# A ring of weight slots at a pitch of 2080 bytes in place of 2048, in a hybrid decoder layer

## The chip, the cores and the metric

The kernel runs on one core of a Trainium2 chip. The engines are named as the profile names them: PE is TensorE with its matmuls (PEld its weight loads), ACT is ScalarE, DVE is VectorE, POOL is GpSimd, SP is the engine that issues most transfers. The metric is the device time of one execution in microseconds; lower is better.

## The reference

One layer of a decoder trunk for 512 positions and a model width of 1024, in float32. A short gated convolution and a gated delta rule run side by side, are merged by sigmoid gates, and a gated feed-forward part with a convolution follows.

```python
h = rmsnorm(x, norm_mix_g)
proj = h @ w_in                                   # 1024 -> nine groups of 1024, and a, b
bg, cg, xv, q, k, v, z, a, b, ga, gb = split(proj)
y_a = (bg * causal_dwconv(cg * xv, conv_a_w)) @ w_a_out
y_b = gdn_branch(q, k, v, z, a, b, ...) @ w_b_out # conv, silu, chunked delta rule, norm, silu(z)
x = x + (sigmoid(ga) * y_a + sigmoid(gb) * y_b) @ w_o
h = rmsnorm(x, norm_ffn_g)
up = causal_dwconv(h @ w_up, ffn_conv_w)          # 1024 -> 2 x 2816
gate, val = split(up)
x = x + (silu(gate) * val) @ w_down
return rmsnorm(x, norm_final_g)
```

## The kernel before

Every large product is split in three. A float32 operand is taken apart into a rounded part, of type float32r, and the remainder; `mm3` sums hi x lo, lo x hi and hi x hi in one bank of PSUM. All of these matmuls are recorded by the helper `mm`, line 108, so line 108 stands for nearly the whole of the kernel's arithmetic. In a row of the profile such as `ps<-hT,wh` the first operand after the arrow is the moving one, the second the stationary one (it is loaded by a LDWEIGHTS of its own).

The activations of a stage lie in SBUF in both parts for the stage's whole length: hT (normalised input, two tiles for the two parts), ts and us (sums and differences of blocks of it, 256 columns wide), yas and yb (the two mixers' outputs), h (the normalised input of the feed-forward part), mix and xs (inputs of the last two products). Weights are streamed. A `Block` is one transfer of 1 MB into one of two `raw` buffers. `Block.part` makes of a quarter of it (128 partitions by 512 elements, 2048 bytes a partition) a rounded copy `wh` on ACT (line 140) and a remainder `wl` on DVE (line 141). wh and wl come from rings of WQ = 12 slots each, in the tile pool `wp`. In the projections the ring's slots are the stationary operand, 128 columns (512 bytes) at a time; in the products with w_o and w_down a slot is the moving operand with all its 512 columns. Some blocks are used by a seven-product scheme (`SumBlock`, L161 and `sum_job`), with products of 256 columns on ts or us.

The order is written out by hand: `run_jobs` goes through a list of jobs, splits the next block while the matmuls of the present one run, and every 4 x 512 columns `tick` advances queues of small steps (evictions, convolutions, the delta rule). A convolution (`conv`, L335 and L338) writes to a buffer named cv: ACT copies the PSUM bank into it, scaled, DVE adds three shifted taps, ACT reads it back through Silu (L973). Three cv buffers are in the pool `gd`; one of them serves `gates_chain` first, under the name abT.

Addresses follow from the order in which the pools hand out space from the bottom of a partition. `const` comes first, with `gate`, a small tile that POOL writes to; then `wp` with raw, the slots of wh and those of wl; then hp (hT, yb), gs, gd, or fp (h) in their place later. The pool `sc` and the later `up` (ts, us, yas, mix, xs) are set from the other end of the partition. `before` and `after` in this table are the byte at which a buffer begins in a partition, in the built program, and behind it what is left on division by 128:

| buffer | before | after |
|---|---|---|
| ident, in const | 1216 (64) | 1248 (96) |
| raw | 2848, 11040 (32) | 2880, 11072 (64) |
| wh, 12 slots | 19232, 21280, 23328, 25376 ... (32 each) | 19264, 21344, 23424, 25504 ... (64, 96, 0, 32, and so on) |
| wl, 12 slots | 43808, 45856 ... (32 each) | 44224, 46304 ... (64, 96, 0, 32, and so on) |
| hT, both parts; later yb in both parts | 68384, 84768 (32) | 69184, 85568 (64) |
| h, both parts | 84768, 101152 (32) | 85568, 101952 (64) |
| ts, yas, mix | 135136, 151520 (96) | the same |
| us, xs | 151520, 167904 (96) | the same |

Within hT, yb and h the k-tiles stand 2048 bytes apart, so each begins at the same remainder; halves of 256 columns do too, and so do ts, us and xs in their steps of 1024 or 512 bytes.

Of the kernel before, what the change touches and what calls it, by code (L numbers as in the profile page):

```python
# [9 lines left out]
F32 = mybir.dt.float32  # L10
F32R = mybir.dt.float32r
# [5 lines left out]
P = 128  # L17
S = 512
# [13 lines left out]
WQ = 12  # L32
# [28 lines left out]
def layer_kernel(ctx, tc, x, norm_mix_g, w_in, w_ab, conv_a_w, gdn_conv_w, gdn_A_log, gdn_dt_bias,  # L61
# [9 lines left out]
    const = ctx.enter_context(tc.tile_pool(name="const", bufs=1))  # L71
    wp = ctx.enter_context(tc.tile_pool(name="wp", bufs=2))
# [3 lines left out]
    def nm(s):  # L76
        cnt[0] += 1
        return f"{s}{cnt[0]}"

    def bank():  # L80
        return ps.tile([P, 512], F32, tag="ps", name=nm("ps"))
# [40 lines left out]
            mm(o, ah, bh, False, i == n - 1, free)  # L122


    class Block:
        def __init__(self, src, quarter=(4, P)):
            self.src, self.quarter = src, quarter
            self.raw, self.ready, self.lead, self.fed = None, False, 2, True
            self.wh, self.wl = {}, {}
# [5 lines left out]
            nc.sync.dma_start(out=self.raw, in_=self.src())  # L135

        def part(self, name, src):
            wh = self.wh[name] = wp.tile([P, *self.quarter], F32R, tag="wh", bufs=WQ, name=nm("wh"))
            wl = self.wl[name] = wp.tile([P, *self.quarter], F32R, tag="wl", bufs=WQ, name=nm("wl"))
            act.copy(out=wh, in_=src)  # L140
            dve.tensor_tensor(out=wl, in0=src, in1=wh.bitcast(F32), op=ALU.subtract)  # L141

# [73 lines left out]
            use(block.wh, block.wl)  # L216


    gate = const.tile([1, 16], F32, name="gate")

    def feed(raw):
        el = raw[0:1, 1].rearrange("p k n -> p (k n)") if len(raw.shape) == 4 else raw[0:1, 1]
# [152 lines left out]
    k_block = Block(lambda: w_in[C_K])  # L375
# [51 lines left out]
    with tc.tile_pool(name="st1", bufs=1) as st1:  # L427
# [83 lines left out]
                                     op0=ALU.mult, op1=ALU.subtract)  # L511

        def round_k(q):
            wh = k_block.wh[q] = wp.tile([P, 4, P], F32R, tag="wh", bufs=WQ, name=nm("wh"))
            act.copy(out=wh, in_=k_block.raw[:, q])

        def rest_k(q):
            wl = k_block.wl[q] = wp.tile([P, 4, P], F32R, tag="wl", bufs=WQ, name=nm("wl"))
            dve.tensor_tensor(out=wl, in0=k_block.raw[:, q], in1=k_block.wh[q].bitcast(F32), op=ALU.subtract)


# [68 lines left out]
    gd = p2.enter_context(tc.tile_pool(name="gd", bufs=1))  # L590

    def hn(ap):
        return ap.rearrange("p (h n) -> p h n", n=NT)

    def prep(pr):
        Dm = gd.tile([P, 8, P], F32, tag="Dm", name=nm("Dm"))
        nc.sync.dma_start(out=Dm, in_=gtd[8 * pr:8 * pr + 8, :].partition_broadcast(P))
        pool.affine_select(out=Dm, in_=Dm, compare_op=ALU.is_ge, fill=-1e30, base=0,
                           pattern=[[0, 8], [1, P]], channel_multiplier=-1)
        Dms[pr] = Dm  # L600
# [8 lines left out]
    Dms = {}  # L609

    def gates_chain(o):
        abT = gd.tile([P, S], F32, tag="cv", bufs=3, name="abT")[0:32]
        act.copy(out=abT, in_=o[0:32, :])
        yield
        o2 = bank()
        for n in range(NT):
            pe.transpose(out=o2[:, n * 32:(n + 1) * 32], in_=abT[:, n * P:(n + 1) * P], identity=ident[:32, :32])
        ab4 = o2[:, 0:128].rearrange("p (n c) -> p c n", c=32)
        abv = gd.tile([P, 16, NT], F32, name="abv")
        dve.tensor_copy(out=abv, in_=ab4[:, 16:32])  # L620
        dve.tensor_tensor(out=abv, in0=abv, in1=ab4[:, 0:16], op=ALU.add)
        T = lambda n: gd.tile([P, 32], F32, tag=n, name=nm(n))
        u, t, z, q, g = T("u"), T("t"), T("z"), T("q"), T("g")
        dve.tensor_tensor(out=hn(u), in0=abv[:, 0:8, :], in1=dtb.unsqueeze(2).broadcast_to([P, H, NT]), op=ALU.add)
        tc.keep_in_program_order(act.activation(out=hn(beta), in_=abv[:, 8:16, :], func=AF.Exp, scale=-1.0))
        tc.keep_in_program_order(act.activation(out=alg, in_=alg, func=AF.Exp))
        dve.tensor_scalar(t, u, -1.0, None, op0=ALU.mult)
        dve.tensor_tensor(out=t, in0=t, in1=u, op=ALU.min)
        tc.keep_in_program_order(act.activation(out=t, in_=t, func=AF.Exp))
        yield  # L630
        pool.tensor_scalar(beta, beta, 1.0, None, op0=ALU.add)
        pool.tensor_scalar(z, t, 2.0, None, op0=ALU.add)
        yield
        dve.reciprocal(out=beta, in_=beta)
        dve.reciprocal(out=z, in_=z)
        dve.tensor_scalar(u, u, 0.0, None, op0=ALU.max)
        yield
        pool.tensor_tensor(out=t, in0=t, in1=z, op=ALU.mult)
        pool.tensor_tensor(out=z, in0=t, in1=t, op=ALU.mult)
        pool.tensor_scalar(q, z, 1.0 / 15.0, 1.0 / 13.0, op0=ALU.mult, op1=ALU.add)  # L640
        for c in (11, 9, 7, 5, 3, 1):
            pool.tensor_tensor(out=q, in0=q, in1=z, op=ALU.mult)
            pool.tensor_scalar(q, q, 1.0 / c, None, op0=ALU.add)
        pool.tensor_tensor(out=q, in0=q, in1=t, op=ALU.mult)
        pool.tensor_scalar(q, q, 2.0, None, op0=ALU.mult)
        pool.tensor_tensor(out=g, in0=q, in1=u, op=ALU.add)
        pool.tensor_tensor(out=hn(g), in0=hn(g), in1=alg.unsqueeze(2).broadcast_to([P, H, NT]), op=ALU.mult)
        pool.tensor_scalar(g, g, -1.0, None, op0=ALU.mult)
        for _ in range(Y_G):
            yield  # L650
        o3 = bank()
        pe.matmul(o3[:, 0:32], lhsT=triu, rhs=g, start=True, stop=True)
        pe.matmul(o3[:, 32:64], lhsT=ones, rhs=g, start=True, stop=True)
        G, Gl = T("G"), T("Gl")
        dve.tensor_copy(out=G, in_=o3[:, 0:32])
        dve.tensor_copy(out=Gl, in_=o3[:, 32:64])
        dve.tensor_scalar(negG, G, -1.0, None, op0=ALU.mult)
        dve.tensor_tensor(out=kdv, in0=Gl, in1=G, op=ALU.subtract)
        act.activation(out=kdv, in_=kdv, func=AF.Exp)
        act.activation(out=eGl, in_=Gl, func=AF.Exp)  # L660
        act.activation(out=eG, in_=G, func=AF.Exp)
        dve.tensor_scalar(neG, eG, -1.0, None, op0=ALU.mult)
        yield
        o4 = bank()
        pe.transpose(out=o4[0:32, 0:P], in_=G, identity=ident)
        GT = gd.tile([32, P], F32, name="GT")
        dve.tensor_copy(out=GT, in_=o4[0:32, 0:P])
        nc.sync.dma_start(out=gtd, in_=GT)
        prep(0)
# [288 lines left out]
    def pair_jobs(pr):  # L958
        st = {}

        def qkv(which, j, o):
            c = gd.tile([P, S], F32, tag="cv", bufs=3, name=nm("cv"))
            yield from conv(c, o, gdn_w(which * 8 + 2 * pr + j), 4)
            if which == 1 and j == 0:
                reach(pr - 2, 99)
                st["kq"] = gd.tile([P, 2, 2, S], F32, tag="kq", bufs=2, name=nm("kq"))
                st["kqs"] = hp.tile([P, 2, 2, 2, S], F32R, tag="s", name=nm("kqs"))
            if which == 2 and j == 0:
                if pr:
                    ftask[pr - 1].until(VREAD)  # L970
                st["vT"] = gd.tile([P, 2, S], F32, tag="vT", name=nm("vT"))
            dst = (lambda: st["kq"][:, j, 1, :], lambda: st["kq"][:, j, 0, :], lambda: st["vT"][:, j, :])[which]()
            act.activation(out=dst, in_=c, func=AF.Silu)  # L973
            yield
            if which < 2:
                hi, lo = (st["kqs"][:, i, j, 1 - which, :] for i in range(2))
                act.copy(out=hi, in_=dst)
                dve.tensor_tensor(out=lo, in0=dst, in1=hi.bitcast(F32), op=ALU.subtract)
                yield
            if which == 2 and j == 1:  # L980
                st["v"] = True
            if which == 0 and j == 1:
                ftask[pr] = Task(front(pr, st))
                chains.append(ftask[pr])

        def zc(j, o):
            act.activation(out=yb[:, 2 * pr + j, :], in_=o, func=AF.Silu)
            if j == 1:
                st["z"] = True
            yield  # L990

        def first_k(wh, wl):
            use_ab()
            for j in range(2):
                products(o_k[j], wh, wl, j, hT, HS, S)
                evacs.append(Task(qkv(1, j, o_k[j])))

        return [(k_block, first_k) if pr == 0 else col_job(w_in, C_K + pr, hT, lambda j, o: qkv(1, j, o)),
                col_job(w_in, C_Q + pr, hT, lambda j, o: qkv(0, j, o)),
                col_job(w_in, C_V + pr, hT, lambda j, o: qkv(2, j, o)),  # L1000
                col_job(w_in, C_Z + pr, hT, zc)]
# [675 lines left out]
```

## Time and profile before

| | |
|---|---|
| three runs | 964.16, 964.42 and 3432.96 us |
| median of the runs | 964.42 us |
| the profiled execution, its own time | 964.32 us |
| its span, first to last instruction | 962.4 us |
| granted TensorE clock, mean | 0.998 of full |

Stages, by the span: the input norm and first projections up to about 25 us; projections for the delta rule beside its chain up to about 340 us; the short convolution's projections on hT and ts up to about 480 us; the two mixers' output products (yas, yb) up to about 595 us; the product with w_o and the second norm up to about 630 us; the feed-forward projections on h and us up to about 848 us; the product with w_down to the end.

In a row of instruction groups stand: line, engine, operation, output<-inputs by the program's names, their sizes, the count; behind the bar the busy time and the mean duration in ns; behind the second bar the idle time of that engine just before them and what ended it. In the timeline a row is the start, the time that it lasts, and how many equal neighbours were merged. Matmuls overlap and their ends are modelled, so their durations are longer than the distance from one start to the next.

### The profile page before, as it was taken

The numbers are of one execution on the slowest core, as the hardware profiler recorded it, in microseconds if no ns is written. First come the engines' busy times: TensorE is split into PE (matmuls) and PEld (weight loads), VectorE is DVE, ScalarE is ACT, GpSimd is POOL, SyncE is SP. The second block draws the span as 40 slices with busy tenths as digits, with TensorE's granted clock in tenths as the row PEclk, the third lists the DMA queues.
The fourth block names the chain that finished last, engine by engine and source line by source line (L and its number), as shares of the span: only waits on it lengthen the run. The fifth ranks groups of instructions, "written<-read, shape, count | busy, mean of one in ns | idle before, by whom it ended". The sixth has DMA issues, their size and how long they took to land.

```text
span 962.4 us, 16188 instructions
## 1 busy us (share of the span) xinstructions
PE 951.7 (99%) x6188; PEld 822.9 (86%) x6188; DVE 743.4 (77%) x1401; ACT 506.6 (53%) x1073; POOL 150.5 (16%) x251
## 2 busy tenths in 40 slices
PE   8999999999999999999999999999999999999997
PEld 7888887987878889999988888998889999888885
DVE  6878686896725958799863479999988888969775
ACT  7895556565444434344741235645645456546463
POOL 3330300202000102311231100221222210000000
PEclk9999999999999999999999999999999999999999
DMA  6544312213221456756787435594774683176342
GB/s 227 160 135 123 94 53 89 75 54 95 53 89 45 140 134 144 181 156 165 239 255 163 120 107 222 153 230 159 178 195 163 196 162 131 45 261 230 99 131 88
DMA packets 51629, 138.11 MB, mean 144 GB/s; under 512 B 21691, under 2 KB 22112, under 8 KB 42848
## 3 DMA queue, kind: packets, MB, share of 16 engines
q1 hardware_dynamic: 38864, 107.45, 33.1%
q0 software_dynamic: 12544, 29.37, 15.9%
q8 instruction: 48, 0.79, 0.3%
q14 instruction: 29, 0.24, 0.1%
q10 hardware_dynamic: 144, 0.26, 0.1%
HBM read 133.64 MB, written 32.78 MB: 173 GB/s over the span
## 4 chain that ended last, share of the span: by engine, by line
PE 91%; DVE 4%; ACT 1%; issue 1%; POOL 1%; POOLq 0%
PE ps L108 83%; PE ps L689 1%; PE ps L724 1%; DVE wl L141 1%; PE ps L898 1%; PE ps L918 1%; DVE h L1335 1%; PE ps L907 0%; DVE hn L1321 0%; PE ps L886 0%; PE ps L885 0%; PE ps L862 0%; PE ps L856 0%; POOL r L1319 0%; PE ps L800 0%
## 5 line engine op out<-in xcount | busy, mean ns | idle before, releaser
L108 PE MATMUL ps<-hT,wh 128*128 128x512 f32 (+1 forms) x1104 | 318.2, 368 | 0.3 <-DVE hT L509 0.3
L140 ACT CAST wh<-raw 128x512 fp32r<-128x512 f32 x350 | 202.9, 618 | 218.3 <-PE ps L108 145.2
L141 DVE TENSOR_TENSOR wl<-raw,wh 128x512 fp32r<-128x512 f32 x350 | 232.0, 688 | 58.5 <-ACT wh L140 57.3
L108 PEld LDWEIGHTS ps<-hT,wh 128*128 128x128 f32 x1104 | 196.6, 189 | 29.0 <-DVE hT L509 0.5
L108 PE MATMUL ps<-hT,wl 128*128 128x512 f32 (+1 forms) x552 | 195.0, 361 | 0.0
L108 PE MATMUL ps<-h,wh 128*128 128x512 f32 (+1 forms) x704 | 177.7, 341 | 0.3 <-DVE h L1335 0.3
L108 PEld LDWEIGHTS ps<-h,wh 128*128 128x128 f32 x704 | 122.3, 189 | 15.5 <-DVE h L1335 0.5
L108 PEld LDWEIGHTS ps<-hT,wl 128*128 128x128 f32 x552 | 104.3, 189 | 13.8
L108 PE MATMUL ps<-h,wl 128*128 128x512 f32 (+1 forms) x352 | 114.5, 341 | 0.0
L108 PE MATMUL ps<-wh,xs 128*128 128x512 f32 (+1 forms) x320 | 96.9, 384 | 0.0
L108 PEld LDWEIGHTS ps<-h,wl 128*128 128x128 f32 x352 | 66.6, 189 | 7.6
L108 PEld LDWEIGHTS ps<-wh,xs 128*128 128x128 f32 x320 | 59.6, 188 | 13.1
L108 PE MATMUL ps<-wl,xs 128*128 128x512 f32 (+1 forms) x160 | 62.1, 388 | 0.0
L338 DVE SCALAR_TENSOR_TENSOR cv<-ps,wA,cv 128x511 f32<-128x511 f32 (+2 forms) x72 | 53.2, 741 | 4.1 <-ACT cv L335 3.9
L108 PE MATMUL ps<-ts,wh 128*128 128x256 f32 x320 | 56.2, 276 | 0.0
L223 POOL COPY gate<-raw 1x1 f32<-1x1 f32 x38 | 12.9, 338 | 276.0 <-DMA raw<-in_w_in_dram 121.4
L140 ACT CAST wh<-raws 128x512 fp32r<-128x512 f32 x66 | 39.1, 618 | 26.9 <-PE ps L108 8.9
L141 DVE TENSOR_TENSOR wl<-raws,wh 128x512 fp32r<-128x512 f32 x66 | 42.9, 685 | 12.5 <-ACT wh L140 12.3
L161 DVE TENSOR_TENSOR raw<-raw 128x512 f32<-128x512 f32 x72 | 49.4, 686 | 1.4
L108 PEld LDWEIGHTS ps<-ts,wh 128*128 128x128 f32 x320 | 49.0, 188 | 0.0
L108 PE MATMUL ps<-us,wh 128*128 128x256 f32 x256 | 45.0, 276 | 0.0
L108 PE MATMUL ps<-yas,wh 128*128 128x512 f32 x128 | 40.3, 394 | 0.0
(316 smaller groups left out, 1548.5 us busy)
## 6 DMA issues: line engine op xcount, KB each, us to landing
raw<-in_w_in_dram SPq DMA_DIRECT2D x35, 1024.0 KB, 5.1
raw<-in_w_up_dram SPq DMA_DIRECT2D x22, 1024.0 KB, 5.1
dv<-in_w_down_dram POOLq DMA_DIRECT2D x50, 256.0 KB, 6.2
raws<-dv SPq DMA_DIRECT2D x8, 768.0 KB, 5.8
ov<-in_w_o_dram POOLq DMA_DIRECT2D x20, 256.0 KB, 5.1
raws<-in_w_down_dram SPq DMA_DIRECT2D x10, 512.0 KB, 6.1
raw<-in_w_a_out_dram SPq DMA_DIRECT2D x4, 1024.0 KB
raw<-in_w_b_out_dram SPq DMA_DIRECT2D x4, 1024.0 KB, 5.8
```

The lines of the kernel that those rows point to most:

```text
L108: pe.matmul(o, lhsT=a, rhs=b, start=start, stop=stop, skip_group_check=free)
L140: act.copy(out=wh, in_=src)
L141: dve.tensor_tensor(out=wl, in0=src, in1=wh.bitcast(F32), op=ALU.subtract)
L161: dve.tensor_tensor(out=r[q], in0=a, in1=b, op=op)
L223: tc.keep_in_program_order(pool.tensor_copy(out=gate[:, 0:1], in_=el[:, 0:1]))
L338: dve.scalar_tensor_tensor(out=dst[:, sh:], in0=src[:, :S - sh], scalar=wcol(j), in1=dst[:, sh:], op0=ALU.mult, op1=ALU.add)
L689: pe.transpose(out=o[:, n * P:(n + 1) * P], in_=src[:, n * P:(n + 1) * P], identity=ident)
L724: pe.matmul(o[:, i], lhsT=kqs[:, a, h, 0, sl], rhs=kqs[:, b, h, :, sl], start=a > 0, stop=a + b == 0)
L898: pe.matmul(o[:, 0:P], lhsT=TTf[:, f, :], rhs=rs[h], start=True, stop=True)
L918: pe.matmul(o[:, 0:P], lhsT=A[:, f, :], rhs=vns[h], start=True, stop=True)
L1335: dve.tensor_tensor(out=h2[1][:, 4 * g:4 * g + 4, t * P:(t + 1) * P], in0=ov, in1=hs.bitcast(F32), op=ALU.subtract)
```

## The change

A helper `slot` takes the place of the four tile requests for wh and wl. It asks for 520 elements and hands on the first 512, so that slots stand 2080 bytes apart. `gate` grows from 16 to 24 elements, which lifts all that follows it by 32 bytes. To make room for the 24 x 32 + 32 = 800 bytes, the pool `gd` has two cv buffers, not three.

```diff
+    PITCH = 520
+
+    def slot(tag, *dims):
+        t = wp.tile([P, PITCH], F32R, tag=tag, bufs=WQ, name=nm(tag))[:, 0:4 * P]
+        return t.rearrange("p (a b) -> p a b", a=dims[0]) if len(dims) == 2 else t
+
...
         def part(self, name, src):
-            wh = self.wh[name] = wp.tile([P, *self.quarter], F32R, tag="wh", bufs=WQ, name=nm("wh"))
-            wl = self.wl[name] = wp.tile([P, *self.quarter], F32R, tag="wl", bufs=WQ, name=nm("wl"))
+            wh = self.wh[name] = slot("wh", *self.quarter)
+            wl = self.wl[name] = slot("wl", *self.quarter)
...
-    gate = const.tile([1, 16], F32, name="gate")
+    gate = const.tile([1, 24], F32, name="gate")
...
         def round_k(q):
-            wh = k_block.wh[q] = wp.tile([P, 4, P], F32R, tag="wh", bufs=WQ, name=nm("wh"))
+            wh = k_block.wh[q] = slot("wh", 4, P)
...
         def rest_k(q):
-            wl = k_block.wl[q] = wp.tile([P, 4, P], F32R, tag="wl", bufs=WQ, name=nm("wl"))
+            wl = k_block.wl[q] = slot("wl", 4, P)
...
     def gates_chain(o):
-        abT = gd.tile([P, S], F32, tag="cv", bufs=3, name="abT")[0:32]
+        abT = gd.tile([P, S], F32, tag="cv", bufs=2, name="abT")[0:32]
...
-            c = gd.tile([P, S], F32, tag="cv", bufs=3, name=nm("cv"))
+            c = gd.tile([P, S], F32, tag="cv", bufs=2, name=nm("cv"))
```

On all five engines the instructions stand in the same order as before, with the same operands. One wait differs. It is on ACT, in the first convolutions of the delta rule's part, where the buffers cv_493 and cv_546 take the two halves of the first k projection. Before:

```order
L140 CAST wh_578<-raw_401 128x512
L335 ACTIVATE cv_493<-ps_209,wA 128x512 [waits PE_49]
L625 ACTIVATE beta<-abv 128x32 [waits DVE_49]
L626 ACTIVATE alg<-alg 128x8 [waits DMAHW7_49]
L629 ACTIVATE t_458<-t_458 128x32 [waits DVE_49]
L335 ACTIVATE cv_546<-ps_210,wA 128x512 [waits PE_49]
L140 CAST wh_634<-raw_539 128x512 [waits DMAHW1_49]
```

And now (the lines have moved by six):

```order
L146 CAST wh_578<-raw_401 128x512
L341 ACTIVATE cv_493<-ps_209,wA 128x512 [waits PE_49]
L631 ACTIVATE beta<-abv 128x32 [waits DVE_49]
L632 ACTIVATE alg<-alg 128x8 [waits DMAHW7_49]
L635 ACTIVATE t_458<-t_458 128x32 [waits DVE_49]
L341 ACTIVATE cv_546<-ps_210,wA 128x512 [waits PE_49,Activation_49]
L146 CAST wh_634<-raw_539 128x512 [waits DMAHW1_49]
```

Nothing moved; the copy into cv_546, which now takes the buffer that abT had, also waits for an earlier instruction of ACT.

## The prediction

> **What bounds the kernel now.** I read the page first: the share of each engine, then the chain that ended last.
>
> ```profile
> span 962.4 us, 16188 instructions
> PE 951.7 (99%) x6188; PEld 822.9 (86%) x6188; DVE 743.4 (77%) x1401; ACT 506.6 (53%) x1073; POOL 150.5 (16%) x251
> ...
> PE 91%; DVE 4%; ACT 1%; issue 1%; POOL 1%; POOLq 0%
> PE ps L108 83%; PE ps L689 1%; PE ps L724 1%; DVE wl L141 1%; PE ps L898 1%; PE ps L918 1%; DVE h L1335 1%; PE ps L907 0%; DVE hn L1321 0%; PE ps L886 0%; PE ps L885 0%; PE ps L862 0%; PE ps L856 0%; POOL r L1319 0%; PE ps L800 0%
> ```
>
> TensorE holds 91% of the chain, and 83% are the matmuls of line 108. The view of waits, for TensorE alone, says that they hardly ever wait for data:
>
> ```profile
> PE ps L474 <- DVE warm L431: 1.5, 1, 1.5
> ...
> PE ps L108 <- DVE h L1335: 0.3, 1, 0.3
> PE ps L108 <- DVE hT L509: 0.3, 1, 0.3
> ```
>
> So the time is the number of these matmuls times the distance between two starts. The mean durations in the groups are of no use for that, since matmuls overlap (the ends are modelled); the groups give the counts, by moving operand and width, in the order moving, stationary:
>
> ```profile
> L108 PE MATMUL ps<-hT,wh 128*128 128x512 f32 x800 | 260.4, 400 | 0.0
> L108 PE MATMUL ps<-hT,wl 128*128 128x512 f32 x400 | 156.6, 392 | 0.0
> L108 PE MATMUL ps<-h,wh 128*128 128x512 f32 x384 | 119.8, 389 | 0.0
> L108 PE MATMUL ps<-wh,xs 128*128 128x512 f32 x304 | 94.1, 390 | 0.0
> L108 PE MATMUL ps<-h,wl 128*128 128x512 f32 x192 | 74.8, 390 | 0.0
> L108 PE MATMUL ps<-h,wh 128*128 128x256 f32 x320 | 60.7, 284 | 0.3 <-DVE h L1335 0.3
> L108 PE MATMUL ps<-wl,xs 128*128 128x512 f32 x152 | 59.9, 394 | 0.0
> L108 PE MATMUL ps<-hT,wh 128*128 128x256 f32 x304 | 58.9, 284 | 0.3 <-DVE hT L509 0.3
> L108 PE MATMUL ps<-ts,wh 128*128 128x256 f32 x320 | 56.2, 276 | 0.0
> L108 PE MATMUL ps<-us,wh 128*128 128x256 f32 x256 | 45.0, 276 | 0.0
> ...
> L108 PE MATMUL ps<-h,wl 128*128 128x256 f32 x160 | 39.7, 282 | 0.0
> L108 PE MATMUL ps<-yb,wh 128*128 128x512 f32 x128 | 39.6, 389 | 0.0
> L108 PE MATMUL ps<-hT,wl 128*128 128x256 f32 x152 | 38.4, 282 | 0.0
> L108 PE MATMUL ps<-ts,wl 128*128 128x256 f32 x160 | 38.4, 276 | 0.0
> L108 PE MATMUL ps<-us,wl 128*128 128x256 f32 x128 | 30.7, 276 | 0.0
> ...
> L108 PE MATMUL ps<-yb,wl 128*128 128x512 f32 x64 | 24.9, 389 | 0.0
> ```
>
> The distances come from the timeline of TensorE (start, duration, count of equal neighbours), at four places where nothing but line 108 runs:
>
> ```profile
> 527.98 2.03 PE L108 MATMUL ps<-yas,wh 128*128 128x512 f32 x8
> 529.85 0.39 PE L108 MATMUL ps<-yb,wh 128*128 128x512 f32 x1
> ...
> 632.34 1.24 PE L108 MATMUL ps<-h,wh 128*128 128x256 f32 x9
> 633.42 0.28 PE L108 MATMUL ps<-h,wl 128*128 128x256 f32 x1
> ...
> 648.16 2.20 PE L108 MATMUL ps<-h,wh 128*128 128x512 f32 x9
> 650.20 0.39 PE L108 MATMUL ps<-h,wl 128*128 128x512 f32 x1
> ...
> 663.78 0.28 PE L108 MATMUL ps<-us,wl 128*128 128x256 f32 x1
> 665.93 0.28 PE L108 MATMUL ps<-us,wh 128*128 128x256 f32 x1
> ...
> 854.99 0.39 PE L108 MATMUL ps<-wl,xs 128*128 128x512 f32 x1
> 869.41 0.39 PE L108 MATMUL ps<-wl,xs 128*128 128x512 f32 x1
> ```
>
> Reading them: h at 512 columns 2.04 us for 9, 226.7 ns each; h at 256 1.08 us for 9, 120.0 ns; us at 256 2.15 us for 19, 113.2 ns; yas at 512 1.87 us for 8, 233.8 ns; wh and wl against xs 14.42 us for 63 (21 times one wl and two wh), 228.9 ns. From h: 256 more columns cost 106.7 ns, 0.417 ns a column, so 512 columns are 213.3 ns and 256 are 106.7. Each matmul then pays 6.5 to 20 ns over its columns, and that surcharge differs between matmuls of the same shape and type. What differs is where the operands lie. By the table of addresses, h and hT begin 32 bytes past a multiple of 128, us and yas 96 past; the ring's slots 32 past, xs 96 past. The distances 113.2, 120.0, 226.7 and 233.8 are 17, 18, 34 and 35 steps of 6.67 ns, within 0.5 ns, and one step is the time of 16 columns, 64 bytes. I take it that a stream is fetched in pieces of 64 bytes: 32 bytes off, 512 columns touch 33 pieces and 256 touch 17, and most pay one or two steps above that. This is inferred; no moving float32r operand of this kernel begins on a multiple of 64.
>
> **The change, part by part.** The order and number of instructions stay the same on all engines, so no work is added; the addresses move, and one wait appears.
>
> Two convolution buffers. The one new wait is the ACT copy of the second k tile (line 335) on an earlier instruction of ACT itself, the write of abT, which stands far ahead of it in the same queue; the wait for TensorE that it had already (PE_49) is unchanged. Behind it on ACT stand the roundings of line 140 and the Silu of line 973. Cost 0: cover is the queue's own order. Without it, the price would be one copy of 0.68 us:
>
> ```profile
> L335 ACT ACTIVATE cv<-ps,wA x24: 665/682/700, 26.6 to 226.0; 128x512 f32<-128x512 f32 x24
> ```
>
> Roundings and remainders that fill the ring (lines 140, 141) are written to other addresses. VectorE shows no dependence on them, and it is idle for 9% of its busiest long stage, so I cost it at 0, covered by the matmuls it runs beside:
>
> ```profile
> L141 DVE TENSOR_TENSOR wl<-raw,wh 128x512 fp32r<-128x512 f32 x350 | 232.0, 688 | 58.5 <-ACT wh L140 57.3
> L1423 DVE TENSOR_TENSOR aTa<-v,g 128x512 f32<-128x512 f32 x14 | 9.6, 688 | 0.2
> 635.00:840.00 205.00, 205.00 (x1250) 183.70 (x1249) 186.51 (x291) 110.94 (x191) 33.91 (x58) 1.00 0.58 156
> ```
>
> (688 ns with an output 32 past a multiple of 128, 688 with one 96 past. The last row is a stretch of the view by windows: TensorE busy 205.0 of 205 us, VectorE 186.5.)
>
> Moving operands. hT, yb and h go from 32 to 64 past, on a multiple of 64. That concerns 800+400+384+192+128+64 = 1968 matmuls of 512 columns and 320+304+160+152 = 936 of 256. Nothing in the trace shows this placing, so the price is bounded from rows: at best the surcharge vanishes, 13.4 ns less at both widths; at worst 512 columns go to the 233.8 of yas, 7.1 ns more, while 256 stay at 120.0, the slowest seen. I take one step of 6.67 ns less: the stream then touches 32 or 16 pieces, one fewer than now, and what is left of the surcharge (one step) stays. That is 1968 x 6.67 = 13.1 us and 936 x 6.67 = 6.2 us. us, ts and yas don't move. The ring as moving operand (xs, 304+152 matmuls; the smaller mix groups are left out) is on a multiple of 64 in every other slot: 228 x 6.67 = 1.5 us.
>
> Stationary operands. The slots lie 64, 96, 0, 32 past, by turns, so a quarter each is 0, 32, 64 and 96 bytes from the residue of h. The trace knows two distances. 512 columns: 226.7 at equal residues, 228.9 at 64 apart (xs), 2.2 more; I take half of it on average, 1968 x 1.1 = 2.2 us lost. 256 columns: 120.0 at equal residues, 113.2 at 64 apart. So ts and us (320+256+160+128 = 864) can lose their good place in a quarter of the cases: 864 x 6.8 / 4 = 1.5 us lost. Ends: 0 and 2.2 ns at 512 (4.3 us), 0 and 6.8 ns at 256 (5.9 us).
>
> Sum: 13.1 + 6.2 + 1.5 - 2.2 - 1.5 = 17.1 us less. The profiled execution took 964.3 us (span 962.4 and 1.9 around it), the median is 964.4: 947.2, I say 947.
>
> **The rivals.**
>
> Two steps fall, not one: the surcharge of aligned streams vanishes. Then another 19.4 us go, 2904 x 6.67: 928. For it: h sits at 34 and 18 steps, two above its 32 and 16 full pieces, so two are there to lose. Against: no matmul of line 108 shows that, and in the stretch above VectorE's 186.5 us of work would face a TensorE of about 191 us, so some waits would appear. The Trainium skill (TensorE: Matmul & The Clock Gate, Back-to-back issue gap) gives N/2.4 + 2.5 ns, 215.8 and 109.2 ns; taken for hT, yb and h alone, an estimate of 21.5 + 10.1 = 31.6 us less, 933. The trace disagrees with that for every address it holds, by 10.9 ns at h with 512 columns.
>
> The placing does nothing: the distances belong to the matmul's kind (which buffer, which neighbours), not to its address. Then all terms are 0: 964. For it: no two rows differ in address alone; us is laid out in other blocks than h. Against: h and yas are the same shape and type with the same stationary ring, and 7.1 ns apart. The Trainium skill (TensorE: Matmul & The Clock Gate, Step-by-step: what each phase is for) speaks for this rival: TensorE reads moving data and weights through two independent ports, and loading the next weights takes nothing from the running matmul. By it the new residues of the slots would cost nothing, and it names no address.
>
> Slower: equal residues of stream and weights are what keeps h at 34 steps, and the wandering slots lose it. Place: line 108 in all stages with hT, yb and h at 512 columns, and ts, us at 256. Price: 1968 x 7.1 = 14.0 us and 864 x 6.8 = 5.9 us, together 984. It decides as soon as the loss per matmul is above what alignment gains: with no gain, each ns at 512 columns costs 2.0 us. For it: xs, 64 apart, is slower than h. Against: yas is 64 apart and us too, and they lie on both sides of h.
>
> **How the numbers follow.** One step less 0.42, by itself 938 to 956 (stationary ends 0 to 10.2 us, and half a step on 2904 matmuls to either side taken in part); two steps 0.20, 924 to 938; nothing 0.20, 961 to 967; slower 0.18, 967 to 984. The prediction is that of the first, 947. The range 926 to 975 leaves out less than 0.05 below and about 0.09 above. 2% is 19.3 us, about what a measurement of this kernel can tell from no change: faster needs less than 945.1. The first case gives 0.17 of its 0.42 to faster and 0.25 to the same; two steps 0.20 to faster; nothing 0.20 to the same; slower 0.10 to the same and 0.08 to slower. Sums: 0.37, 0.55, 0.08.
>
> **What would show it.** Distances in the timeline of TensorE: h, hT and yb at 512 columns near 220 ns and at 256 near 113.3 show the step; 213 and 107 show two; 226.7 and 120 show that placing does nothing; 230 and more show the slower rival. yas should stay within 227 to 234, us within 113 to 120. If quarters of the ring differ, distances change with the slot of the next weights; if only the start counts, they don't. The line of waits should keep no new wait of line 108 over 1 us; if VectorE's remainders (line 141) appear there, the gain is capped by supply. The prediction is wrong at its root if distances of aligned streams are not shorter, or if waits rather than distances carry the difference.

## The result, and the profile after

The changed kernel takes 976.99 us (median of 3 runs, 976.18 to 977.39) against 964.42 before: a ratio of 1.0128 [1.0114, 1.0143], slower by 1.3%. That is inside 2%, but far more than the 0.1% by which the runs that enter the ratio differ among each other (the run of 3432.96 us of the kernel before does not enter it). 947.0 was forecast with a range of 926 to 975. So the sign was wrong, and the time lies 2 us above the range.

The page of the changed kernel shows the span, the busy time by engine, the chain that ended last, and, among the groups, that of the remainders wl on VectorE:

```profile
span 974.7 us, 16189 instructions
...
PE 964.0 (99%) x6188; PEld 825.8 (85%) x6188; DVE 745.7 (77%) x1401; ACT 508.4 (52%) x1073; POOL 151.7 (16%) x251
...
PE 91%; DVE 4%; ACT 1%; issue 1%; POOL 1%; POOLq 0%
PE ps L108 83%; PE ps L695 1%; PE ps L730 1%; DVE wl L147 1%; PE ps L904 1%; PE ps L924 1%; DVE h L1341 0%; PE ps L913 0%; DVE hn L1327 0%; PE ps L892 0%; PE ps L891 0%; PE ps L862 0%; PE ps L868 0%; POOL r L1325 0%; PE ps L806 0%
...
L147 DVE TENSOR_TENSOR wl<-raw,wh 128x512 fp32r<-128x512 f32 x350 | 233.7, 692 | 61.4 <-ACT wh L146 60.4
```

The chain reads as before, 91% TensorE and 83% line 108, with the same 6188 matmuls. TensorE's busy time has grown by 12.3 us, as much as the span (962.4 to 974.7). The remainders on VectorE grew by 4 ns each, beside matmuls that last longer.

The waits of TensorE in the changed kernel, with the total, the number and the longest in us:

```profile
PE ps L480 <- DVE warm L437: 1.5, 1, 1.5
PE ps L508 <- DVE xr L503: 1.0, 2, 0.8
PE ps L695 <- DVE vs L943: 0.5, 1, 0.5
PE ps L108 <- DVE h L1341: 0.3, 1, 0.3
PE ps L108 <- DVE hT L515: 0.3, 1, 0.3
```

Line 108 has the same two waits of 0.3 us as before. The time is not in waits, so it must be in the distance from one matmul's start to the next. To read that closely, take long stretches where only line 108 runs. The first is the two mixers' products: 192 matmuls on yas, then 192 on yb, then the first on mix (so the product with w_o begins at 573 us of the kernel before, earlier than the 595 us that the list of stages gives). The second is 48 matmuls of 256 columns on us, followed by h. In the timeline of TensorE of the kernel before these stretches begin at

```profile
485.05 0.39 PE L108 MATMUL ps<-yas,wh 128*128 128x512 f32 x1
...
573.38 0.39 PE L108 MATMUL ps<-wh,mix 128*128 128x512 f32 x1
...
662.28 0.29 PE L108 MATMUL ps<-us,wh 128*128 128x256 f32 x1
...
667.74 0.28 PE L108 MATMUL ps<-h,wh 128*128 128x256 f32 x1
```

(the first on yb is at 529.85, a row that the prediction quotes), and in the timeline of the changed kernel, with two starts on xs that are 60 matmuls apart, at

```profile
491.24 0.40 PE L108 MATMUL ps<-yas,wh 128*128 128x512 f32 x1
...
535.71 0.39 PE L108 MATMUL ps<-yb,wh 128*128 128x512 f32 x1
...
580.25 0.40 PE L108 MATMUL ps<-wh,mix 128*128 128x512 f32 x1
...
669.72 0.28 PE L108 MATMUL ps<-us,wh 128*128 128x256 f32 x1
...
675.40 0.28 PE L108 MATMUL ps<-h,wh 128*128 128x256 f32 x1
...
869.57 0.39 PE L108 MATMUL ps<-wl,xs 128*128 128x512 f32 x1
...
883.48 0.40 PE L108 MATMUL ps<-wl,xs 128*128 128x512 f32 x1
```

A stretch divided by its count gives the distance. yas goes from 233.3 to 231.6 ns, yb from 226.7 to 232.0, us from 113.8 to 118.3, xs from 228.9 (the prediction's reading) to 231.8. What had been 226.7, 228.9 and 233.3 at 512 columns is now 232 for all. (The prediction's 233.8 for yas and 113.2 for us came from 8 and 19 matmuls; over the longer stretches they are 233.3 and 113.8.) The next table sums the distances from one matmul of line 108 to the next, over the whole trace and by the first one's moving operand; the rest is distances that begin or end at another line, and the 24 matmuls of 256 columns on xs, 2.7 us in both kernels, are left out. It shows where the 12.3 us went:

| moving operand | before, us | after, us | difference |
|---|---|---|---|
| hT, h and yb, 512 columns | 433.1 | 441.0 | +7.9 |
| ts and us, 256 columns | 98.3 | 101.9 | +3.6 |
| wh and wl (on xs and mix), 512 columns | 142.2 | 143.9 | +1.7 |
| yas, 512 columns | 44.8 | 44.5 | -0.3 |
| hT and h, 256 columns | 116.6 | 115.5 | -1.1 |
| the rest | 115.7 | 116.2 | +0.5 |

### The profile page after: what moved, and what is told of

Same layout as the page of the kernel before. It is cut to its first block, busy times and chain, and to the rows that moved or that the text cites. A ratio compares the mean times of both kernels' runs of the same rounds, so it can differ in the third digit from the quotient of the medians.

```text
span 974.7 us, 16189 instructions
## 1 busy us (share of the span) xinstructions
PE 964.0 (99%) x6188; PEld 825.8 (85%) x6188; DVE 745.7 (77%) x1401; ACT 508.4 (52%) x1073; POOL 151.7 (16%) x251
## 4 chain that ended last, share of the span: by engine, by line
PE 91%; DVE 4%; ACT 1%; issue 1%; POOL 1%; POOLq 0%
PE ps L108 83%; PE ps L695 1%; PE ps L730 1%; DVE wl L147 1%; PE ps L904 1%; PE ps L924 1%; DVE h L1341 0%; PE ps L913 0%; DVE hn L1327 0%; PE ps L892 0%; PE ps L891 0%; PE ps L862 0%; PE ps L868 0%; POOL r L1325 0%; PE ps L806 0%
## 5 line engine op out<-in xcount | busy, mean ns | idle before, releaser
L108 PE MATMUL ps<-ts,wh 128*128 128x256 f32 x320 | 58.3, 280 | 0.0
L147 DVE TENSOR_TENSOR wl<-raws,wh 128x512 fp32r<-128x512 f32 x66 | 43.0, 686 | 13.1 <-ACT wh L146 13.0
L108 PE MATMUL ps<-yb,wh 128*128 128x512 f32 x128 | 40.2, 394 | 0.0
```

Source lines behind the costliest of these rows:

```text
L108: pe.matmul(o, lhsT=a, rhs=b, start=start, stop=stop, skip_group_check=free)
```

## The experiments

Theory at the start: a distance is a fixed whole number of steps of 6.67 ns as long as the moving operand and the stationary operand that is loaded beside it keep one relation of their addresses, and the pitch of 2080 bytes breaks that. Rivals: the placing of the moving operand alone, which the shift by 32 bytes changes; the third convolution buffer with its wait; the pitch of the slots itself. The diffs are against the changed kernel. For brevity, "remainder" below is the moving operand's address less the stationary operand's. In the kernel before it is 0 for hT, h and yb (all 32 past a multiple of 256, as the slots are), 192 for ts, us and yas, and 64 for the slots against xs and mix, on division by 256. The distances come from the starts in each kernel's timeline.

### One part of the change at a time

Only the convolution buffers (e1_cv_only):

```diff
-    PITCH = 520
+    PITCH = 512
-    gate = const.tile([1, 24], F32, name="gate")
+    gate = const.tile([1, 16], F32, name="gate")
```

> Two convolution buffers alone, pitch 2048, nothing shifted. Wandering residues (the theory: the distance of two matmuls is a fixed whole number of 6.67 ns steps as long as stream and weights keep one residue each, and the pitch of 2080 breaks that): 964 us, as before. Placing of the streams: 964. Buffers and the new wait (rival): 977, as with the whole change.

It took 964.16 us against 964.38, 0.9996 [0.9987, 1.0006]. The third buffer and its wait are worth nothing.

Buffers and shift, old pitch (e2_shift_only): now slots, hT, h and yb all begin on a multiple of 64, and stay at remainder 0 to each other, while ts, us, yas, mix and xs stay where they were.

```diff
-    PITCH = 520
+    PITCH = 512
```

> Pitch 2048 and two convolution buffers, with the ring and all above it 32 bytes higher: hT, h and yb begin 64 past a multiple of 128, all slots too. Wandering residues: every distance is one whole number of steps again, 512 columns of h at 220, 226.7 or 233.3 ns and not between; 226.7 would be 964 us, 220 about 945, 233.3 about 977. Placing of the streams (the multiple of 64 is itself what costs): h at 232 ns as after the change, 975 to 977 us.

It took 969.94 us, 1.0055 [1.0040, 1.0070]. Its timeline of TensorE, the same starts, the two on xs 60 matmuls apart:

```profile
486.80 0.40 PE L108 MATMUL ps<-yas,wh 128*128 128x512 f32 x1
...
531.78 0.40 PE L108 MATMUL ps<-yb,wh 128*128 128x512 f32 x1
...
575.32 0.39 PE L108 MATMUL ps<-wh,mix 128*128 128x512 f32 x1
...
859.67 0.40 PE L108 MATMUL ps<-wl,xs 128*128 128x512 f32 x1
...
873.67 0.40 PE L108 MATMUL ps<-wl,xs 128*128 128x512 f32 x1
```

yb is at 43.54 us / 192 = 226.8 ns, as when it lay 32 bytes lower: a stream that begins on a multiple of 64 is not faster. What got slower are the products whose other operand did not move: xs from 228.9 to 233.3, and ts and us from 113.7 to 117.4 (means over the trace). There are 617 of the one (with mix) and 864 of the other, 2.7 and 3.1 us, and with 0.2 of yas that makes 6.0, of which 5.6 show. So the expectation was right for yb and missed the time, because it followed hT, h and yb alone; and the part of the theory on whole steps fell, since 117.4 ns is no whole number of them (nor had 228.9 on xs been one).

Buffers and pitch, no shift (e3_pitch_only):

```diff
-    gate = const.tile([1, 24], F32, name="gate")
+    gate = const.tile([1, 16], F32, name="gate")
```

> Pitch 2080 and two convolution buffers, hT, h and yb 32 past a multiple of 128 as before. Wandering residues: distances between whole steps, h at 512 columns near 232 ns, us and ts at 256 near 118, 975 to 979 us. Placing of the streams: h at 226.7, 964 us.

It took 976.1 us, 1.0119 [1.0104, 1.0134]. The pitch alone makes the whole loss, with the ring at either of its two beginnings. The two starts around yb in its timeline of TensorE are 44.56 us apart, 232.1 ns a matmul:

```profile
535.24 0.39 PE L108 MATMUL ps<-yb,wh 128*128 128x512 f32 x1
...
579.80 0.40 PE L108 MATMUL ps<-wh,mix 128*128 128x512 f32 x1
```

### The stream moved against a ring at the old pitch

Here slots stand 2048 bytes apart and begin where they did before; a pad behind the ring lifts what lies above it, of line 108's large operands hT, h and yb alone, so that one fixed remainder holds for all their matmuls. With 16 elements it is 64 (e4_stream_64_up):

```diff
+    ctx.enter_context(tc.tile_pool(name="gap", bufs=1)).tile([P, 16], F32, name="gap")
-    PITCH = 520
+    PITCH = 512
-    gate = const.tile([1, 24], F32, name="gate")
+    gate = const.tile([1, 16], F32, name="gate")
```

> Pitch 2048, slots 32 past a multiple of 128 as before, two convolution buffers, and 64 bytes of gap between the ring and hT: hT, h and yb begin 96 past, as us, ts and yas do. If the step count is set by the pair of residues of stream and weights: h takes what yas and us showed before, 233.3 ns at 512 columns and 113.3 at 256: 1968 x 6.67 more and 936 x 6.67 less, 971 us. If the residue of the weights alone counts, or the buffer and its neighbours: 226.7 and 120, 964 us.

It took 966.39 us, 1.0020 [1.0010, 1.0030], neither of the two times expected. In its timeline of TensorE (the added line makes 108 into 109):

```profile
531.20 0.39 PE L109 MATMUL ps<-yb,wh 128*128 128x512 f32 x1
...
575.15 0.39 PE L109 MATMUL ps<-wh,mix 128*128 128x512 f32 x1
```

That is 228.9 ns; h at 256 columns is at 117.7. The pair of 233.3 and 113.3 that a period of 128 bytes called for did not come. But 228.9 is exactly what the slots against xs have, whose remainder is also 64; yas and us, at 192, are another class. So the period is not 128. It may be 256, which the next three test, by the same edit with a pad of 8, 32 and 56 elements (e5_stream_32_up, e6_stream_128_up, e7_stream_224_up).

> Pitch 2048, slots 32 past a multiple of 128, a gap of 32 bytes between the ring and hT: the streams hT, h and yb begin 32 bytes above the residue of their weights. If the difference of the two addresses, divided by 256, sets the distance (so far: remainder 0 gives 226.7 ns at 512 columns and 120 at 256; 64 gives 228.9 and 117.8; 192 gives 233.3 and 113.5): h, hT and yb change, to something not seen yet, ts, us, yas and xs keep 113.6, 113.6, 233.3 and 228.9. If only the weights' residue counts, all stay and the time is 964 us. If a stream on a multiple of 64 saves a step of 6.67 ns as the prediction had it: 220 and 113.3, 945 us.

> As the run before with a gap of 128 bytes: remainder 128 of 256, 0 of 128. If the pattern repeats every 128 bytes: h, hT and yb at 226.7 and 120 ns, 964 us. If it repeats every 256 bytes: other distances than that. ts, us, yas and xs unchanged in both cases.

> As the two before with a gap of 224 bytes: remainder 224. The pair theory gives a distance of its own to h, hT and yb and leaves ts, us, yas and xs at 113.6, 113.6, 233.3 and 228.9; with 512 columns anywhere from 224 to 236 ns and 256 from 113 to 120, 958 to 983 us. If only the weights' residue counts: 964 us.

They took 973.12 us, 1.0092 [1.0075, 1.0109]; 972.69 us, 1.0084 [1.0069, 1.0099]; and 976.78 us, 1.0126 [1.0111, 1.0141]. The starts around yb in the timeline of the first,

```profile
534.51 0.39 PE L109 MATMUL ps<-yb,wh 128*128 128x512 f32 x1
...
579.31 0.40 PE L109 MATMUL ps<-wh,mix 128*128 128x512 f32 x1
```

of the second,

```profile
534.25 0.39 PE L109 MATMUL ps<-yb,wh 128*128 128x512 f32 x1
...
578.86 0.39 PE L109 MATMUL ps<-wh,mix 128*128 128x512 f32 x1
```

and of the third, here with the stretch on us:

```profile
536.53 0.40 PE L109 MATMUL ps<-yb,wh 128*128 128x512 f32 x1
...
581.33 0.39 PE L109 MATMUL ps<-wh,mix 128*128 128x512 f32 x1
...
670.68 0.28 PE L109 MATMUL ps<-us,wh 128*128 128x256 f32 x1
...
676.33 0.28 PE L109 MATMUL ps<-h,wh 128*128 128x256 f32 x1
```

give 233.3, 232.3 and 233.3 ns for yb. The first of them settles alignment a second time: there the streams begin on a multiple of 64 (64 past one of 256) and are slower than before by 6.6 ns. The second rules out a period of 128: moved by 128 bytes, the stream is at 232.3 and not at 226.8. The third holds a surprise: us, which nothing touched, takes 5.65 us / 48 = 117.7 ns where it took 113.8 and was expected to stay.

Two finer steps, one run each, are 16 and 240 bytes up, with a helper `placed` in place of the pad (e9_stream_16_up with 4 elements, e10_stream_240_up with 60):

```diff
+    def placed(pool, dt, tag, name, off, *dims):
...
+        t = pool.tile([P, n + 64], dt, tag=tag, name=name)[:, off:off + n]
...
-    PITCH = 520
+    PITCH = 512
-    gate = const.tile([1, 24], F32, name="gate")
+    gate = const.tile([1, 16], F32, name="gate")
-    hT = [hp.tile([P, ND, S], F32R, tag=f"h{i}", name=f"hT{i}") for i in range(2)]
+    hT = [placed(hp, F32R, f"h{i}", f"hT{i}", 4, ND, S) for i in range(2)]
...
-        st["yb"] = [hp.tile([P, ND, S], F32R, tag=f"h{i}", name=f"yb{i}") for i in range(2)]
+        st["yb"] = [placed(hp, F32R, f"h{i}", f"yb{i}", 4, ND, S) for i in range(2)]
...
-        st["h2"] = [fp.tile([P, ND, S], F32R, tag=f"h2{i}", name=f"h2{i}") for i in range(2)]
+        st["h2"] = [placed(fp, F32R, f"h2{i}", f"h2{i}", 4, ND, S) for i in range(2)]
...
```

> Pitch 2048; hT, yb and h begin 16 bytes above the residue of the ring (remainder 16 of 256). Pair theory without a law between its points: h, hT and yb away from 226.8 and 120, between 224 and 236 and between 113 and 120. If only multiples of 32 matter: as remainder 0, 964 us.

> As the run before, at remainder 240, 16 bytes below. Pair theory: again distances of its own, 224 to 236 and 113 to 120 ns; if only multiples of 32 matter, 964 us.

They took 973.56 and 976.91 us (the kernel before beside them 964.38). The starts around yb in the timelines of TensorE, first 16 and then 240 bytes up,

```profile
534.76 0.39 PE L116 MATMUL ps<-yb,wh 128*128 128x512 f32 x1
...
579.25 0.39 PE L116 MATMUL ps<-wh,mix 128*128 128x512 f32 x1
```

```profile
536.14 0.39 PE L116 MATMUL ps<-yb,wh 128*128 128x512 f32 x1
...
581.57 0.40 PE L116 MATMUL ps<-wh,mix 128*128 128x512 f32 x1
```

give 231.7 and 236.6 ns, the second just above the 236 that was named as the end. Remainder 0 is no wide valley: 16 bytes to either side cost 5 and 10 ns. Here the helper shifts hT, h and yb within tiles 256 bytes larger, so that nothing else changes its place on division by 256, while the pad moved all that lies above the ring.

### The pitch changed, the remainder kept; and all at remainder 0

If it is the remainder and not the pitch, a pitch of 2304 bytes, nine times 256, should cost nothing (e11_pitch_2304; a slot less wide a ring, 10 in place of 12, makes it fit):

```diff
-WQ = 12
+WQ = 10
-    PITCH = 520
+    PITCH = 576
-    gate = const.tile([1, 24], F32, name="gate")
+    gate = const.tile([1, 16], F32, name="gate")
```

> Pitch 2304, a multiple of 256 larger than 2048, with ten slots in each ring, not twelve, to make room. Slots stand apart, but all at one residue. If the pitch itself (slots not back to back) costs: h, hT and yb near 232 ns at 512 columns, ts and us near 118. If the remainder of the difference by 256 sets the distance: 226.8 and 113.6 as before; waits for a free slot may add to the whole time, not to these distances.

It took 967.86 us in one run. The starts around yb in its timeline of TensorE,

```profile
533.77 0.39 PE L108 MATMUL ps<-yb,wh 128*128 128x512 f32 x1
...
577.31 0.39 PE L108 MATMUL ps<-wh,mix 128*128 128x512 f32 x1
```

are 226.8 ns apart, and us is at 113.7, yas at 233.3: these distances are as before the change. Slots 2304 bytes apart lie by turns at two places on division by 512, so the period is not 512 either. Of the 3.5 us that it is slower, 3.0 are a wait, which heads the view of waits for its TensorE:

```profile
PE ps L108 <- DVE kn L716: 3.0, 1, 3.0
```

Of the kernels here only this one has ten slots; that the shorter ring causes the wait was not tried by itself.

The last run uses what was learned: if 0 is best at 512 columns, yas, mix and xs should lie there too, 64 bytes higher, while ts and us keep 192 (e8_all_at_zero):

```diff
+    def placed(pool, dt, tag, name, off, *dims):
...
-    PITCH = 520
+    PITCH = 512
-    gate = const.tile([1, 24], F32, name="gate")
+    gate = const.tile([1, 16], F32, name="gate")
-        st["ts"] = [sc.tile([P, 4, 4, HS], F32R, tag=f"t{i}", name=f"ts{i}") for i in range(2)]
+        st["ts"] = [placed(sc, F32R, f"t{i}", f"ts{i}", 0, 4, 4, HS) for i in range(2)]
-        st["yas"] = [st["sc"].tile([P, ND, S], F32R, tag=f"t{i}", name=f"yas{i}") for i in range(2)]
+        st["yas"] = [placed(st["sc"], F32R, f"t{i}", f"yas{i}", 16, ND, S) for i in range(2)]
...
-            st["xs"] = [st["up"].tile([P, 4, 4, HS], F32R, tag=f"t{e}", name=f"xs{e}") for e in range(2)]
+            st["xs"] = [placed(st["up"], F32R, f"t{e}", f"xs{e}", 16, 4, 4, HS) for e in range(2)]
```

> Pitch 2048, two convolution buffers, and yas, mix and xs begin 64 bytes further up in their tiles, so that these too differ from the ring by a multiple of 256 (ts and us stay at remainder 192, the best seen for 256 columns). Pair theory: yas from 233.3 to 226.8 ns (192 x 6.5 = 1.2 us), wh and wl against xs and mix from 228.9 to 226.8 (some 588 x 2.1 = 1.2 us): 962 us, below both kernels by 0.25%. If the distance belongs to the buffer and its neighbours: 964 us.

It took 962.19 us against 964.38, 0.9978 [0.9969, 0.9987]: faster than both kernels. Its timeline of TensorE, with two starts on xs 60 matmuls apart:

```profile
485.40 0.39 PE L116 MATMUL ps<-yas,wh 128*128 128x512 f32 x1
...
528.92 0.39 PE L116 MATMUL ps<-yb,wh 128*128 128x512 f32 x1
...
661.13 0.29 PE L116 MATMUL ps<-us,wh 128*128 128x256 f32 x1
...
666.59 0.28 PE L116 MATMUL ps<-h,wh 128*128 128x256 f32 x1
...
851.73 0.39 PE L116 MATMUL ps<-wl,xs 128*128 128x512 f32 x1
...
865.33 0.39 PE L116 MATMUL ps<-wl,xs 128*128 128x512 f32 x1
```

yas stands at 226.7 (233.3 before), the slots against xs at 226.7 (228.9 before), and us at 113.8 as before. 192 x 6.7 and 617 x 2.1 ns are 2.6 us, of which 2.2 show.

### What the runs say together

Distances by remainder on division by 256, means in the named kernels over the stretches where line 108 runs alone. Buffers of one remainder agree within 0.5 ns at 512 columns (at remainder 0 yb has 226.8 and h 227.1); at 256 columns a mean moves by 0.2 with how many of a stretch's first distances are counted:

| remainder | 512 columns, ns | 256 columns, ns | where |
|---|---|---|---|
| 0 | 226.8 | 119.4 | before, e1, e2, e8, e11 |
| 32 | 233.3 | 116.8 | e5 |
| 64 | 229.0 | 117.7 | e4; xs before |
| 96 | 233.3 | 119.8 (23 matmuls only) | xs in e2 |
| 128 | 232.4 | 118.7 | e6 |
| 160 | 234.3 | 117.4 | yas, ts and us in e2 |
| 192 | 233.3 | 113.7, or 117.8 in e7 and e9 | yas, ts and us before |
| 224 | 233.3 | 118.4 | e7 |

A pitch of 2080 bytes goes through all eight in turn, 32 bytes on with each slot. The mean of the column at 512 is 232.0 ns (1855.7 / 8), and at 256 it is 117.7 (with 113.7 at 192); that twelve slots meet four of the eight twice changes neither by more than 0.1. The changed kernel has 232.0 on yb and 118 on the 256-column operands. So the loss is as large as the average over the eight remainders makes it, where the kernel before had two groups of matmuls at the cheapest ones, hT, h and yb at 0 and ts and us at 192.

That the pitch costs its time through the remainder is shown, by e3 and e11 with the steps between them. That each matmul then pays the price of its own remainder is argued from the agreement of the means alone, and the single matmuls of the changed kernel speak against it. Sort its distances on yas and yb by remainder, counting the slots on in the order of use: from whichever of the twelve slots the count starts, and whether the slot of the matmul itself or of the next is taken, the means, over some 45 distances each, lie between 230.8 and 232.9 ns, and none is near 226.8 at remainder 0. On yas and yb the remainder there changes at every second matmul or sooner, while the table comes from streams that keep one. What a matmul takes also hangs on those before it: in the kernel before, yb follows yas at remainder 192, and its first five distances are 226, 236, 228, 232 and 231 ns; in e8 it follows yas at remainder 0, and all 192 are 226 or 227.

What stays open: why the remainder matters. The runs show that the relation of the two operands' addresses sets the distance and that the period is 256 bytes; no view shows the reads themselves. Whether the operand that counts is the one being loaded for the next matmul or the one already loaded was not separated, since a ring at a fixed remainder has both the same. Nor was it settled what chooses between 113.7 and 117.8 ns at remainder 192: in e7 and e9 hT, h and yb have been moved and the address of us has not, and in e4 us changes from the slower to the faster on the way.

## Why the prediction was wrong

- **Two convolution buffers, cost 0**: right. e1 is at 0.9996.
- **Filling the ring, cost 0**: right for the time. The remainders wl went from 688 to 692 ns each and no wait of line 108 appeared.
- **Moving operands, one step of 6.67 ns less each**: this is the step that failed. It was to give 13.1, 6.2 and 1.5 us and gave nothing. From 33 pieces of 64 bytes against 32 it was inferred that alignment sets the surcharge; e2 puts these streams on multiples of 64 and leaves them at 226.8 and about 119.5 ns, and e5, aligned too, makes them slower. The error was in reading two quantities that went together in most rows: yas and us differ from h in their alignment and in their remainder to the ring as well, and the distances 226.7, 228.9 and 233.3 belong to the second. One row did separate the two. The slots that stream against xs begin 32 past a multiple of 128, as h does, and take 228.9 ns to its 226.7; the prediction used that row for the stationary operands and not against its own step. It said that the step was inferred, and yet gave it the largest chance. The rival of two steps rests on the same reading and falls with it.
- **Stationary operands, 2.2 and 1.5 us lost**: the right mechanism, mis-sized. At 512 columns h, hT and yb lost 7.9 us, above the end of 4.3; ts and us 3.6, inside the end of 5.9. The size came from taking addresses on division by 128. By that, xs, yas and us are all 64 away, so that yas and us lay on both sides of h at one remainder, which the prediction held against the slower rival, and xs and yas differed by 4.4 ns; on division by 256 xs is 64 away, yas and us are 192. A price of 2.2 ns at 512 columns is that of the cheapest of the seven unequal remainders in the table; their mean is 5.9.
- **The slower rival**, 984 at a chance of 0.18: its mechanism is the one that holds, equal remainders keep h at 34 steps and wandering slots lose it. It priced every matmul at the worst that the trace had, 7.1 ns; yb lost 5.2, and hT, h and yb together 7.9 us, not 14.0. And it let h and hT at 256 columns go unpriced, which gained 1.1 us.
- **The rival of no effect, by which TensorE reads the two operands independently**: it fell too. With the slots fixed, moving the stream alone by 32 bytes takes yb from 226.8 to 233.3 ns (e5), and moving both together changes nothing (e2). The Trainium skill (TensorE: Matmul & The Clock Gate, Step-by-step: what each phase is for) says that loading the next weights takes no read bandwidth from the running matmul. The distances of e5 disagree with what the rival drew from that, no effect of the addresses on each other; whether read bandwidth is what is lost, no view shows.
- **What would show it**: "230 and more show the slower rival" was the right test, and h and yb answered 232.0; yas (231.6) and us (118.3) lie in the bands named for them, and no wait of line 108 passed 1 us.

## What to carry to other kernels

Where TensorE's matmuls run back to back and the trace shows no wait, compare the distances from start to start between operands of one shape; if they fall into classes, list each operand's address against that of the operand loaded beside it before blaming alignment or buffer. For a ring of weights take a pitch that keeps one remainder for all slots (here a multiple of 256 bytes; 2304 gave the same distances as 2048), then move the streamed tiles against it: here a few pad elements were worth 0.2% against the placing that the kernel before happened to have and 1.5% against the pitch of 2080. Where two properties differ together in most rows of a trace, look for the row that separates them before pricing one; where none does, the range has to hold both readings.

## What the runs showed of the hardware

- The distance of two float32r matmuls in these kernels depends on the difference of the two operands' SBUF addresses on division by 256: 226.8 to 236.6 ns at 512 columns, 113.7 to 119.8 at 256. A shift by 128 bytes changes it (232.3 on yb in e6 against 226.8); slots 2304 bytes apart, which differ by 256 on division by 512, keep it (226.8 in e11).
- The best place is not the same for both widths: at remainder 0, 512 columns are at their fastest and 256 columns near their slowest (119.4); at 192, 512 columns are slow (233.3) and 256 columns at their fastest (113.7).
- At remainder 0 nearly all distances are 34 steps of 6.67 ns (188 of 192 on yb before the change); at remainder 64 those on yb in e4 go between 225 and 232 ns, and only their mean of 228.9 is steady.
- One remainder can run at two speeds: us at remainder 192 takes 113.7 ns on average in e8 and 117.8 in e7, and in e4 it goes over from the slower to the faster on the way.
